# A log-sum-exp over heads: 2 MB loads, the bias of four heads added by TensorE in fp32, halves summed pairwise, last tile in pieces

## The chip, the cores and the metric

The program runs on one core of a Trainium2 chip. The metric is the device time of one execution in microseconds. A run over 1.5% above the fastest of the same kernel counts as slow.

## The reference

```python
B, S, D, H = 8, 2048, 2048, 8          # x: [8, 2048, 2048] fp32, bias: [8, 256] fp32
x_heads = x.reshape(B, S, H, Dh).transpose(0, 2, 1, 3) + bias[None, :, None, :]
x_tiled = np.repeat(x_heads, 2, axis=2)
mx = x_tiled.max(axis=-1, keepdims=True)
lse = mx.squeeze(-1) + np.log(np.exp(x_tiled - mx).sum(axis=-1))
```

For each row and head, 256 numbers are added to a bias, exponentiated and summed; the logarithm of the sum is written twice. The input is 134 MB and is read once, so the kernel is mostly a long stream of loads. Neither kernel subtracts the maximum.

## The kernel before

A tile is 128 rows of 2048 numbers (1 MB). Seven heads go one way: ScalarE takes the exponential in place, VectorE multiplies by exp(bias) and sums. The eighth head goes another way: TensorE adds the bias in PSUM (two bf16 products, reading the upper halves of the fp32 words), and ScalarE exponentiates and sums.

```python
XIN_BUFS = 8
for b in range(B):
    for sblk in range(nsblk):                               # 16 tiles of 1 MB
        xt = xin.tile([P, D], mybir.dt.float32, name="xt")
        nc.sync.dma_start(out=xt, in_=x[b, s0 : s0 + P, :])
        for h in range(n_ttr, H):                           # n_ttr = 7: one head
            ps = pspool.tile([P, Dh], mybir.dt.float32, name="ps")
            nc.tensor.matmul(ps, lhsT=ones_bf[0:1, :], rhs=b_hi, start=True, stop=False)
            nc.tensor.matmul(ps, lhsT=ident_bf[:, :], rhs=x_hi, start=False, stop=True)
            nc.scalar.activation(out=ps, in_=ps, func=ACT.Exp, accum_out=R[...])
        nc.scalar.activation(out=xt[:, 0 : 7 * Dh], in_=xt[:, 0 : 7 * Dh], func=ACT.Exp)
        for h in range(7):
            nc.vector.tensor_tensor_reduce(out=junk, in0=xt[:, sl], in1=w_rep[:, sl],
                op0=ALU.mult, op1=ALU.add, accum_out=R[...], ...)
    nc.tensor.transpose(out=ps, in_=R[:, b]..., identity=ident)   # once per batch
    nc.scalar.activation(out=res, in_=ps_view, func=ACT.Ln)
    # ... store
```

The order of instructions on each engine is not the order of this text: a scheduler decides it.

The softmax here doesn't subtract the row's maximum and nothing guards it: scores larger than these inputs give would overflow.

Of the kernel before, what the change touches and what calls it, by code (L numbers as in the profile page):

```python
# [8 lines left out]

N_TTR_HEADS = 7  # L10

XIN_BUFS = 8


@with_exitstack
def kernel(
    ctx: ExitStack,
    tc: tile.TileContext,
    x: bass.AP,
    bias: bass.AP,  # L20
    out: bass.AP,
):
    nc = tc.nc
    P = nc.NUM_PARTITIONS
    B, S, D = x.shape
    H, Dh = bias.shape
    assert D == H * Dh
    assert S % P == 0
    nsblk = S // P
    NCOL = H * nsblk  # L30
    assert NCOL <= P

    n_ttr = max(0, min(N_TTR_HEADS, H))
    ACT = mybir.ActivationFunctionType
    ALU = mybir.AluOpType

    const = ctx.enter_context(tc.tile_pool(name="const", bufs=1))
    rpool = ctx.enter_context(tc.tile_pool(name="rpool", bufs=1))
    xin = ctx.enter_context(tc.tile_pool(name="xin", bufs=XIN_BUFS))
    junkp = ctx.enter_context(tc.tile_pool(name="junkp", bufs=2))  # L40
    pspool = ctx.enter_context(tc.tile_pool(name="pspool", bufs=3, space=bass.MemoryType.PSUM))
    pspoolw = ctx.enter_context(tc.tile_pool(name="pspoolw", bufs=2, space=bass.MemoryType.PSUM))
    tpsum = ctx.enter_context(tc.tile_pool(name="tpsum", bufs=2, space=bass.MemoryType.PSUM))
    resp = ctx.enter_context(tc.tile_pool(name="resp", bufs=2))

    with tc.high_priority():
        act_sets = list(get_activation_tables(nc.m.arch).items())
        for set_idx, (_set_name, funcs) in enumerate(act_sets):
            if ACT.Exp in funcs and ACT.Ln in funcs:
                nc.scalar.add_instruction(  # L50
                    mybir.InstLoadActFuncSet(
                        name=nc.get_next_instruction_name(),
                        act_func_set_id=set_idx,
                    )
                )
                break

        ident = const.tile([P, P], mybir.dt.float32, name="ident")
        make_identity(nc, ident)
        ident_bf = const.tile([P, P], mybir.dt.bfloat16, name="ident_bf")  # L60
        make_identity(nc, ident_bf)
        ones_bf = const.tile([1, P], mybir.dt.bfloat16, name="ones_bf")
        nc.vector.memset(ones_bf, 1.0)  # L63

        brow = const.tile([1, D], mybir.dt.float32, name="brow")
        nc.scalar.dma_start(
            out=brow, in_=bias.rearrange("h j -> (h j)").unsqueeze(0)
        )
        w_rep = const.tile([P, D], mybir.dt.float32, name="w_rep")
        brb = brow.bitcast(mybir.dt.bfloat16)  # L70
        WCH = 512
        for c in range(D // WCH):
            b_hi_c = bass.AP(
                tensor=brb.tensor,
                offset=brb.offset + 2 * c * WCH + 1,
                ap=[[brb.ap[0][0], 1], [2, WCH]],
            )
            psw = pspoolw.tile([P, WCH], mybir.dt.float32, name="psw")
            nc.tensor.matmul(  # L79
                psw, lhsT=ones_bf[0:1, :], rhs=b_hi_c, start=True, stop=True  # L80
            )
            nc.scalar.activation(  # L82
                out=w_rep[:, c * WCH : (c + 1) * WCH], in_=psw, func=ACT.Exp
            )

    R = rpool.tile([P, B, H, nsblk], mybir.dt.float32, name="R")

    for b in range(B):
        for sblk in range(nsblk):
            s0 = sblk * P  # L90
            xt = xin.tile([P, D], mybir.dt.float32, name="xt")
            nc.sync.dma_start(out=xt, in_=x[b, s0 : s0 + P, :])

            if n_ttr < H:
                xb = xt.bitcast(mybir.dt.bfloat16)
                bb = brow.bitcast(mybir.dt.bfloat16)
            for h in range(n_ttr, H):
                x_hi = bass.AP(
                    tensor=xb.tensor,
                    offset=xb.offset + 2 * h * Dh + 1,  # L100
                    ap=[xb.ap[0], [2, Dh]],
                )
                b_hi = bass.AP(
                    tensor=bb.tensor,
                    offset=bb.offset + 2 * h * Dh + 1,
                    ap=[[bb.ap[0][0], 1], [2, Dh]],
                )
                ps = pspool.tile([P, Dh], mybir.dt.float32, name="ps")
                nc.tensor.matmul(  # L109
                    ps, lhsT=ones_bf[0:1, :], rhs=b_hi, start=True, stop=False  # L110
                )
                nc.tensor.matmul(  # L112
                    ps, lhsT=ident_bf[:, :], rhs=x_hi, start=False, stop=True
                )
                nc.scalar.activation(  # L115
                    out=ps,
                    in_=ps,
                    func=ACT.Exp,
                    accum_out=R[:, b, h, sblk : sblk + 1],
                )  # L120

            if n_ttr > 0:
                nc.scalar.activation(  # L123
                    out=xt[:, 0 : n_ttr * Dh],
                    in_=xt[:, 0 : n_ttr * Dh],
                    func=ACT.Exp,
                )
                for h in range(n_ttr):
                    sl = slice(h * Dh, (h + 1) * Dh)
                    junk = junkp.tile([P, Dh], mybir.dt.float32, name="junk")  # L130
                    nc.vector.tensor_tensor_reduce(  # L131
                        out=junk,
                        in0=xt[:, sl],
                        in1=w_rep[:, sl],
                        scale=1.0,
                        scalar=0.0,
                        op0=ALU.mult,
                        op1=ALU.add,
                        accum_out=R[:, b, h, sblk : sblk + 1],
                    )  # L140

        ps = tpsum.tile([NCOL, P], mybir.dt.float32, name="tps")
        nc.tensor.transpose(  # L143
            out=ps, in_=R[:, b].rearrange("p h s -> p (h s)"), identity=ident
        )
        res = resp.tile([NCOL, P, 2], mybir.dt.float32, name="res")
        ps_view = bass.AP(
            tensor=ps.tensor,
            offset=ps.offset,
            ap=[ps.ap[0], [1, P], [0, 2]],  # L150
        )
        nc.scalar.activation(out=res, in_=ps_view, func=ACT.Ln)  # L152
        ov = bass.AP(
            tensor=out.tensor,
            offset=out.offset + b * H * 2 * S,
            ap=[[2 * P, NCOL], [1, 2 * P]],
        )
        out_eng = nc.sync if b == B - 1 else nc.gpsimd
        out_eng.dma_start(out=ov, in_=res.rearrange("p s e -> p (s e)"))  # L159


# [28 lines left out]
```

## Time and profile before

| | before |
|---|---|
| time, median of the runs beside the changed kernel | 347.40 us |
| profiled span | 345.5 us |
| VectorE busy | 92% |
| ScalarE busy | 79% |
| load rate in the steady part | about 421 GB/s |
| last load complete at (its last packet ended at 336.7) | 337.2 us |

From the page of the kernel before: busy time per engine, then the span in 40 slices, each digit the busy tenths of a slice.

```profile
PE 95.0 (28%) x268; PEld 27.6 (8%) x268; DVE 316.6 (92%) x1793; ACT 272.4 (79%) x397; POOL 5.0 (1%) x15
...
DVE  0899989899898998999989989899899998999985
ACT  4978878788787887878778878788777887878872
...
DMA  7999999999999999999999999999999999999700
GB/s 303 427 421 421 417 422 423 422 421 421 419 423 417 424 421 419 423 420 424 423 418 418 424 420 423 421 422 419 422 416 412 370 401 424 420 411 409 286 24 15
```

The loads never rest, and VectorE (DVE) is nearly full. Which of the two is the bound is told by who waits. From the groups of instructions (busy us, mean ns of one, then the idle time just before them and who ended it):

```profile
L131 DVE CUSTOM_DVE_ANT_0 junk<-xt,w_rep 128x256 f32<-128x256 f32 x896 | 316.3, 422 | 24.0 <-ACT xt L123 15.4
L123 ACT ACTIVATE xt<-xt 128x1792 f32<-128x1792 f32 x128 | 217.2, 1698 | 62.7 <-DMA xt<-in_x_dram 56.2
```

VectorE waits for ScalarE, and ScalarE waits 56 us for loads: the loads bound the kernel. From the timeline of the end (start us, duration us, instruction, idle time before it and what ended it):

```profile
331.34 1.70 ACT L123 ACTIVATE xt<-xt 128x1792 f32<-128x1792 f32 x1 [0.38 <-DMA xt<-in_x_dram]
...
334.78 1.70 ACT L123 ACTIVATE xt<-xt 128x1792 f32<-128x1792 f32 x1 [1.35 <-DMA xt<-in_x_dram]
...
337.24 1.70 ACT L123 ACTIVATE xt<-xt 128x1792 f32<-128x1792 f32 x1 [0.37 <-DMA xt<-in_x_dram]
```

Tiles arrive 2.46 us apart, but one gap here is 3.44 us. Such gaps come about every 22 us. In the packets of the trace, an 8 KB instruction fetch goes ahead of each, and one load packet then takes 0.97 us in place of 0.31. After the last landing the kernel needs some 8 us more.

### The profile page before, as it was taken

Reading aid. Unit: us, or ns where it says so; the run is one execution under the profiler, and the core shown is the slowest. Engines: PE = TensorE matmul, PEld = TensorE weight load, DVE = VectorE, ACT = ScalarE, POOL = GpSimd, SP = SyncE. Lnnn points to the kernel's source line nnn. Section 1 sums busy time; section 2 is a strip of 40 time slices with the busy share of each in tenths; the row PEclk is TensorE's granted clock in tenths of the full one; section 3 lists DMA queues with packets and bytes.
Section 4 is the critical chain, followed back from the end, with each engine's and each line's share of the span. In section 5 each row is a group of like instructions: output and inputs, shape, how many; then the busy total and the mean of one; then the engine's idle time right before and its main releaser. Section 6 shows DMA issues by size and latency. Waiting matters only on the chain. (4 is left out here: it accounts for less than half of the span.)

```text
span 345.5 us, 3541 instructions
## 1 busy us (share of the span) xinstructions
PE 95.0 (28%) x268; PEld 27.6 (8%) x268; DVE 316.6 (92%) x1793; ACT 272.4 (79%) x397; POOL 5.0 (1%) x15
## 2 busy tenths in 40 slices
PE   2423223223322323322332322232223232222220
PEld 0100000000000000000010000000000000000000
DVE  0899989899898998999989989899899998999985
ACT  4978878788787887878778878788777887878872
POOL 1000000000000000000000000000000000000000
DMA  7999999999999999999999999999999999999700
GB/s 303 427 421 421 417 422 423 422 421 421 419 423 417 424 421 419 423 420 424 423 418 418 424 420 423 421 422 419 422 416 412 370 401 424 420 411 409 286 24 15
DMA packets 18939, 135.50 MB, mean 392 GB/s; under 512 B 2177, under 2 KB 2305, under 8 KB 2529
## 3 DMA queue, kind: packets, MB, share of 16 engines
q1 hardware_dynamic: 18576, 134.36, 94.3%
q0 software_dynamic: 336, 0.92, 0.7%
q14 instruction: 23, 0.19, 0.1%
q8 instruction: 2, 0.03, 0.0%
q10 hardware_dynamic: 2, 0.01, 0.0%
HBM read 134.23 MB, written 1.05 MB: 392 GB/s over the span
## 5 line engine op out<-in xcount | busy, mean ns | idle before, releaser
L131 DVE CUSTOM_DVE_ANT_0 junk<-xt,w_rep 128x256 f32<-128x256 f32 x896 | 316.3, 422 | 24.0 <-ACT xt L123 15.4
L123 ACT ACTIVATE xt<-xt 128x1792 f32<-128x1792 f32 x128 | 217.2, 1698 | 62.7 <-DMA xt<-in_x_dram 56.2
L109 PE MATMUL ps<-brow,ones_bf 1*128 1x256 bf16 x128 | 46.9, 368 | 207.6 <-ACT ps L115 207.5
L131 DVE DVE_READ_ACCUMULATOR2_ANT R<- 128x1 f32 x896 | 74.8, 83 | 0.0
L112 PE MATMUL ps<-xt,ident_bf 128*128 128x256 bf16 x128 | 49.3, 385 | 21.4 <-DMA xt<-in_x_dram 21.3
L115 ACT ACTIVATE ps<-ps 128x256 f32<-128x256 f32 x128 | 47.2, 369 | 0.0
L112 PEld LDWEIGHTS <-ident_bf 128*128 128x128 bf16 x128 | 13.2, 104 | 245.2 <-issue 245.2
L115 ACT ACTIVATION_READ_ACCUMULATOR ps<-ps 128x1 f32 x128 | 23.5, 184 | 0.0
L109 PEld LDWEIGHTS <-ones_bf 1*128 1x128 bf16 x128 | 12.5, 98 | 45.6 <-issue 45.6
L152 ACT ACTIVATE res<-tps 128x256 f32<-128x256 f32 x8 | 3.1, 383 | 6.6 <-PE tps L143 6.6
L159 POOL DMA_DIRECT2D out_dram<-res x7 | 3.9, 562 | 295.9 <-ACT res L152 295.9
L143 PE MATMUL tps<-ident,R 128*128 128x128 f32 x8 | 3.6, 452 | 13.8 <-DVE R L131 13.8
L79 PE MATMUL psw<-brow,ones_bf 1*128 1x512 bf16 x4 | 2.4, 601 | 4.2 <-DMA brow<-in_bias_dram 2.4
L143 PEld LDWEIGHTS tps<-ident,R 128*128 128x128 f32 x8 | 1.4, 180 | 19.3 <-issue 15.8
L82 ACT ACTIVATE w_rep<-psw 128x512 f32<-128x512 f32 x4 | 2.3, 593 | 0.0
L50 ACT ACT_TABLE_LOAD x1 | 1.3, 1283 | 0.7 <-PEq L174 0.7
L63 DVE MEMSET ones_bf<- 1x128 bf16 x1 | 0.2, 165 | 0.8 <-PEq L174 0.8
L79 PEld LDWEIGHTS <-ones_bf 1*128 1x128 bf16 x4 | 0.5, 118 | 4.0 <-issue 3.0
masks.py:199 POOL TENSOR_SCALAR_AFFINE_SELECT ident<-ident 128x128 f32<-128x128 f32 x1 | 0.3, 285 | 0.0
masks.py:199 POOL TENSOR_SCALAR_AFFINE_SELECT ident_bf<-ident_bf 128x128 bf16<-128x128 bf16 x1 | 0.3, 285 | 0.0
masks.py:197 POOL MEMSET ident<- 128x128 f32 x1 | 0.2, 205 | 0.3 <-POOLq L174 0.3
masks.py:197 POOL MEMSET ident_bf<- 128x128 bf16 x1 | 0.2, 206 | 0.0
(4 smaller groups left out, 0.4 us busy)
## 6 DMA issues: line engine op xcount, KB each, us to landing
xt<-in_x_dram SPq DMA_DIRECT2D x128, 1024.0 KB, 16.4
out_dram<-res POOLq DMA_DIRECT2D x7, 128.0 KB, 5.8
out_dram<-res SPq DMA_DIRECT2D x1, 128.0 KB
brow<-in_bias_dram ACTq DMA_DIRECT2D x1, 8.0 KB
```

The source lines that it names most:

```text
L50: nc.scalar.add_instruction(mybir.InstLoadActFuncSet(name=nc.get_next_instruction_name(), act_func_set_id=set_idx,))
L63: nc.vector.memset(ones_bf, 1.0)
L79: nc.tensor.matmul(psw, lhsT=ones_bf[0:1, :], rhs=b_hi_c, start=True, stop=True)
L82: nc.scalar.activation(out=w_rep[:, c * WCH : (c + 1) * WCH], in_=psw, func=ACT.Exp)
L109: nc.tensor.matmul(ps, lhsT=ones_bf[0:1, :], rhs=b_hi, start=True, stop=False)
L112: nc.tensor.matmul(ps, lhsT=ident_bf[:, :], rhs=x_hi, start=False, stop=True)
L115: nc.scalar.activation(out=ps, in_=ps, func=ACT.Exp, accum_out=R[:, b, h, sblk : sblk + 1],)
L123: nc.scalar.activation(out=xt[:, 0 : n_ttr * Dh], in_=xt[:, 0 : n_ttr * Dh], func=ACT.Exp,)
L131: nc.vector.tensor_tensor_reduce(out=junk, in0=xt[:, sl], in1=w_rep[:, sl], scale=1.0, scalar=0.0, op0=ALU.mult, op1=ALU.add, accum_out=R[ ...
L143: nc.tensor.transpose(out=ps, in_=R[:, b].rearrange("p h s -> p (h s)"), identity=ident)
L152: nc.scalar.activation(out=res, in_=ps_view, func=ACT.Ln)
L159: out_eng.dma_start(out=ov, in_=res.rearrange("p s e -> p (s e)"))
```

## The change

Its intent: load 2 MB at a time with two rows per partition, so that each packet is longer; take work from VectorE by letting TensorE add the bias of four heads exactly (the fp32 data times an fp32 identity, and the bias split into three bf16 parts), so that VectorE sums their two halves pairwise in half the elements; load the last tile in pieces to shorten the end.

```diff
-N_TTR_HEADS = 7
-XIN_BUFS = 8
+K = 2
+NPE = 4
+XIN_BUFS = 9
 ...
+    pbias = ... tc.tile_pool(name="pbias", bufs=3, space=bass.MemoryType.PSUM)
+        # bias split into three bf16 parts by GpSimd, moved to b3 by three small DMAs
+        nc.gpsimd.tensor_copy(bparts[:, 0], bp)
+        nc.gpsimd.tensor_sub(brest[:, 0], bp, bparts[:, 0])
+        ...
+    def biased(xt, b, blk, k):
+        ps = pbias.tile([P, CPE], F32, name="ps")
+        for c in range(0, CPE, MM):                     # CPE = 1024, MM = 512
+            nc.tensor.matmul(ps[:, c : c + MM], lhsT=ones3, rhs=b3[:, c : c + MM],
+                start=True, stop=False)
+        for c in range(0, CPE, MM):
+            nc.tensor.matmul(ps[:, c : c + MM], lhsT=ident, rhs=xt[:, k, c : c + MM],
+                start=False, stop=True)
+        nc.scalar.activation(out=xt[:, k, 0:CPE], in_=ps, func=ACT.Exp)
+        for h in range(NPE):                            # halves, 128 elements
+            nc.vector.tensor_tensor_reduce(out=junk[:, 0:HALF], in0=xt[:, k, c : c + HALF],
+                in1=xt[:, k, c + HALF : c + Dh], op0=ALU.add, op1=ALU.add, ...)
 ...
+            if not last:
+                nc.sync.dma_start(out=xt, in_=xb[blk])              # 2 MB
+                nc.scalar.activation(out=xt[:, :, CPE:D], in_=xt[:, :, CPE:D], func=ACT.Exp)
+                for k in range(K):
+                    biased(xt, b, blk, k)
+                for k in range(K):
+                    for h in range(NPE, H):
+                        weigh(xt, b, blk, k, h)                     # as before, 256 elements
+            else:
+                # the same in five pieces: 2 x 512 KB for TensorE's heads, 512 KB, 2 x 256 KB
```

More of the change, by code (lines that the diff above doesn't have):

```diff
@@ L8 @@
 from concourse.masks import make_identity
-N_TTR_HEADS = 7
-XIN_BUFS = 8
+F32 = mybir.dt.float32
+BF16 = mybir.dt.bfloat16
+ACT = mybir.ActivationFunctionType
+ALU = mybir.AluOpType
+K = 2
+NPE = 4
+XIN_BUFS = 9
 @with_exitstack
@@ L26 @@
     H, Dh = bias.shape
-    assert D == H * Dh
-    assert S % P == 0
-    nsblk = S // P
-    NCOL = H * nsblk
-    assert NCOL <= P
-    n_ttr = max(0, min(N_TTR_HEADS, H))
-    ACT = mybir.ActivationFunctionType
-    ALU = mybir.AluOpType
+    assert D == H * Dh and S % (P * K) == 0
+    NBLK = S // (P * K)
+    NW = H - NPE
+    CPE = NPE * Dh
+    CW = NW * Dh
+    MM = 512
+    HALF = Dh // 2
     const = ctx.enter_context(tc.tile_pool(name="const", bufs=1))
-    rpool = ctx.enter_context(tc.tile_pool(name="rpool", bufs=1))
     xin = ctx.enter_context(tc.tile_pool(name="xin", bufs=XIN_BUFS))
     junkp = ctx.enter_context(tc.tile_pool(name="junkp", bufs=2))
-    pspool = ctx.enter_context(tc.tile_pool(name="pspool", bufs=3, space=bass.MemoryType.PSUM))
-    pspoolw = ctx.enter_context(tc.tile_pool(name="pspoolw", bufs=2, space=bass.MemoryType.PSUM))
-    tpsum = ctx.enter_context(tc.tile_pool(name="tpsum", bufs=2, space=bass.MemoryType.PSUM))
-    resp = ctx.enter_context(tc.tile_pool(name="resp", bufs=2))
+    pbias = ctx.enter_context(
+        tc.tile_pool(name="pbias", bufs=3, space=bass.MemoryType.PSUM)
+    )
+    tpsum = ctx.enter_context(
+        tc.tile_pool(name="tpsum", bufs=2, space=bass.MemoryType.PSUM)
+    )
+    resp = ctx.enter_context(tc.tile_pool(name="resp", bufs=2))
+    brow = const.tile([1, D], F32, name="brow")
+    w_rep = const.tile([P, CW], F32, name="w_rep")
+    ident = const.tile([P, P], F32, name="ident")
+    ones = const.tile([1, P], F32, name="ones")
+    ones3 = const.tile([3, P], BF16, name="ones3")
+    b3 = const.tile([3, CPE], BF16, name="b3")
+    bparts = const.tile([1, 3, CPE], BF16, name="bparts")
+    brest = const.tile([1, 2, CPE], F32, name="brest")
+    R = const.tile([P, B, K, H, NBLK], F32, name="R")
     with tc.high_priority():
-        act_sets = list(get_activation_tables(nc.m.arch).items())
-        for set_idx, (_set_name, funcs) in enumerate(act_sets):
+        for set_idx, (_name, funcs) in enumerate(
+            get_activation_tables(nc.m.arch).items()
+        ):
             if ACT.Exp in funcs and ACT.Ln in funcs:
@@ L56 @@
                 break
-        ident = const.tile([P, P], mybir.dt.float32, name="ident")
-        make_identity(nc, ident)
-        ident_bf = const.tile([P, P], mybir.dt.bfloat16, name="ident_bf")
-        make_identity(nc, ident_bf)
-        ones_bf = const.tile([1, P], mybir.dt.bfloat16, name="ones_bf")
-        nc.vector.memset(ones_bf, 1.0)
-        brow = const.tile([1, D], mybir.dt.float32, name="brow")
         nc.scalar.dma_start(
@@ L68 @@
         )
-        w_rep = const.tile([P, D], mybir.dt.float32, name="w_rep")
-        brb = brow.bitcast(mybir.dt.bfloat16)
-        WCH = 512
-        for c in range(D // WCH):
-            b_hi_c = bass.AP(
-                tensor=brb.tensor,
-                offset=brb.offset + 2 * c * WCH + 1,
-                ap=[[brb.ap[0][0], 1], [2, WCH]],
-            )
-            psw = pspoolw.tile([P, WCH], mybir.dt.float32, name="psw")
-            nc.tensor.matmul(
-                psw, lhsT=ones_bf[0:1, :], rhs=b_hi_c, start=True, stop=True
-            )
-            nc.scalar.activation(
-                out=w_rep[:, c * WCH : (c + 1) * WCH], in_=psw, func=ACT.Exp
-            )
@@ L86 @@
-    R = rpool.tile([P, B, H, nsblk], mybir.dt.float32, name="R")
-    for b in range(B):
-        for sblk in range(nsblk):
-            s0 = sblk * P
-            xt = xin.tile([P, D], mybir.dt.float32, name="xt")
-            nc.sync.dma_start(out=xt, in_=x[b, s0 : s0 + P, :])
-            if n_ttr < H:
-                xb = xt.bitcast(mybir.dt.bfloat16)
-                bb = brow.bitcast(mybir.dt.bfloat16)
-            for h in range(n_ttr, H):
-                x_hi = bass.AP(
-                    tensor=xb.tensor,
-                    offset=xb.offset + 2 * h * Dh + 1,
-                    ap=[xb.ap[0], [2, Dh]],
-                )
-                b_hi = bass.AP(
-                    tensor=bb.tensor,
-                    offset=bb.offset + 2 * h * Dh + 1,
-                    ap=[[bb.ap[0][0], 1], [2, Dh]],
-                )
-                ps = pspool.tile([P, Dh], mybir.dt.float32, name="ps")
-                nc.tensor.matmul(
-                    ps, lhsT=ones_bf[0:1, :], rhs=b_hi, start=True, stop=False
-                )
-                nc.tensor.matmul(
-                    ps, lhsT=ident_bf[:, :], rhs=x_hi, start=False, stop=True
-                )
-                nc.scalar.activation(
-                    out=ps,
-                    in_=ps,
-                    func=ACT.Exp,
-                    accum_out=R[:, b, h, sblk : sblk + 1],
-                )
-            if n_ttr > 0:
-                nc.scalar.activation(
-                    out=xt[:, 0 : n_ttr * Dh],
-                    in_=xt[:, 0 : n_ttr * Dh],
-                    func=ACT.Exp,
-                )
-                for h in range(n_ttr):
-                    sl = slice(h * Dh, (h + 1) * Dh)
-                    junk = junkp.tile([P, Dh], mybir.dt.float32, name="junk")
-                    nc.vector.tensor_tensor_reduce(
-                        out=junk,
-                        in0=xt[:, sl],
-                        in1=w_rep[:, sl],
-                        scale=1.0,
-                        scalar=0.0,
-                        op0=ALU.mult,
-                        op1=ALU.add,
-                        accum_out=R[:, b, h, sblk : sblk + 1],
-                    )
-        ps = tpsum.tile([NCOL, P], mybir.dt.float32, name="tps")
-        nc.tensor.transpose(
-            out=ps, in_=R[:, b].rearrange("p h s -> p (h s)"), identity=ident
-        )
-        res = resp.tile([NCOL, P, 2], mybir.dt.float32, name="res")
-        ps_view = bass.AP(
-            tensor=ps.tensor,
-            offset=ps.offset,
-            ap=[ps.ap[0], [1, P], [0, 2]],
-        )
-        nc.scalar.activation(out=res, in_=ps_view, func=ACT.Ln)
@@ new lines @@
+        nc.vector.memset(ones, 1.0)
+        nc.vector.memset(ones3, 1.0)
+        make_identity(nc, ident)
+        psw = pbias.tile([P, CW], F32, name="ps")
+        for c in range(0, CW, MM):
+            nc.tensor.matmul(
+                psw[:, c : c + MM],
+                lhsT=ones,
+                rhs=brow[:, CPE + c : CPE + c + MM],
+                start=True,
+                stop=True,
+            )
+        nc.scalar.activation(out=w_rep, in_=psw, func=ACT.Exp)
+        bp = brow[:, 0:CPE]
@@ new lines @@
+        nc.gpsimd.tensor_copy(bparts[:, 0], bp)
+        nc.gpsimd.tensor_sub(brest[:, 0], bp, bparts[:, 0])
+        nc.gpsimd.tensor_copy(bparts[:, 1], brest[:, 0])
+        nc.gpsimd.tensor_sub(brest[:, 1], brest[:, 0], bparts[:, 1])
+        nc.gpsimd.tensor_copy(bparts[:, 2], brest[:, 1])
+        for i in range(3):
+            nc.gpsimd.dma_start(out=b3[i : i + 1, :], in_=bparts[:, i])
+    def biased(xt, b, blk, k):
+        ps = pbias.tile([P, CPE], F32, name="ps")
+        for c in range(0, CPE, MM):
+            nc.tensor.matmul(
+                ps[:, c : c + MM],
+                lhsT=ones3,
+                rhs=b3[:, c : c + MM],
+                start=True,
+                stop=False,
+            )
+        for c in range(0, CPE, MM):
+            nc.tensor.matmul(
+                ps[:, c : c + MM],
+                lhsT=ident,
+                rhs=xt[:, k, c : c + MM],
+                start=False,
+                stop=True,
+            )
+        nc.scalar.activation(out=xt[:, k, 0:CPE], in_=ps, func=ACT.Exp)
+        for h in range(NPE):
+            c = h * Dh
+            junk = junkp.tile([P, Dh], F32, name="junk")
+            nc.vector.tensor_tensor_reduce(
+                out=junk[:, 0:HALF],
+                in0=xt[:, k, c : c + HALF],
+                in1=xt[:, k, c + HALF : c + Dh],
+                scale=1.0,
+                scalar=0.0,
+                op0=ALU.add,
+                op1=ALU.add,
+                accum_out=R[:, b, k, h, blk : blk + 1],
+            )
@@ new lines, in weigh @@
+    def weigh(xt, b, blk, k, h):
+        c = h * Dh
+        junk = junkp.tile([P, Dh], F32, name="junk")
+        nc.vector.tensor_tensor_reduce(
+            out=junk,
+            in0=xt[:, k, c : c + Dh],
+            in1=w_rep[:, c - CPE : c - CPE + Dh],
+            scale=1.0,
+            scalar=0.0,
+            op0=ALU.mult,
+            op1=ALU.add,
+            accum_out=R[:, b, k, h, blk : blk + 1],
+        )
+    for b in range(B):
+        xb = x[b].rearrange("(n p k) d -> n p k d", p=P, k=K)
+        for blk in range(NBLK):
+            xt = xin.tile([P, K, D], F32, name="xt")
+            last = b == B - 1 and blk == NBLK - 1
+            if not last:
+                nc.sync.dma_start(out=xt, in_=xb[blk])
+                nc.scalar.activation(
+                    out=xt[:, :, CPE:D], in_=xt[:, :, CPE:D], func=ACT.Exp
+                )
+                for k in range(K):
[4 more added lines that the diff above has]
+            else:
+                pieces = [(k, 0, CPE) for k in range(K)]
+                pieces += [(k, CPE, D) for k in range(K - 1)]
+                pieces += [(K - 1, CPE + i * MM, CPE + (i + 1) * MM) for i in range(CW // MM)]
+                for k, c0, c1 in pieces:
+                    nc.sync.dma_start(
+                        out=xt[:, k, c0:c1], in_=xb[blk, :, k, c0:c1]
+                    )
+                for k, c0, c1 in pieces:
+                    if c0 < CPE:
+                        biased(xt, b, blk, k)
+                        continue
+                    for c in range(c0, c1, MM):
+                        nc.scalar.activation(
+                            out=xt[:, k, c : c + MM],
+                            in_=xt[:, k, c : c + MM],
+                            func=ACT.Exp,
+                        )
+                        for h in range(c // Dh, (c + MM) // Dh):
+                            weigh(xt, b, blk, k, h)
+        NR = H * NBLK
+        tps = tpsum.tile([NR, K, P], F32, name="tps")
+        for k in range(K):
+            nc.tensor.transpose(
+                out=tps[:, k],
+                in_=R[:, b, k].rearrange("p h n -> p (h n)"),
+                identity=ident,
+            )
+        res = resp.tile([NR, P, K, 2], F32, name="res")
+        tv = bass.AP(
+            tensor=tps.tensor,
+            offset=tps.offset,
+            ap=[tps.ap[0], [1, P], [P, K], [0, 2]],
+        )
+        nc.scalar.activation(out=res, in_=tv, func=ACT.Ln)
@@ L155 @@
             offset=out.offset + b * H * 2 * S,
-            ap=[[2 * P, NCOL], [1, 2 * P]],
+            ap=[[2 * K * P, NR], [1, 2 * K * P]],
         )
         out_eng = nc.sync if b == B - 1 else nc.gpsimd
-        out_eng.dma_start(out=ov, in_=res.rearrange("p s e -> p (s e)"))
+        out_eng.dma_start(out=ov, in_=res.rearrange("p s k e -> p (s k e)"))
 _INS = ['x', 'bias']
```

## The prediction

> **What bounds it now.** The loads, and among the 16 DMA engines the slowest one. The slices show 421 GB/s and DMA at 9 tenths nearly throughout; the page has VectorE 92% busy, ScalarE 79%. ScalarE's big exponentials start 2.48 us apart (1 MB at 421 GB/s), except about every 22 us, when the gap is 3.45 us. In the trace's packets an instruction fetch (8 KB, 0.33 us) precedes each such gap, and one 8 KB load packet then takes 0.97 us in place of 0.31. The engine that carries these fetches falls behind: 15 of the 16 parts of the last tile land by 327.8 us, the last at 337.2 us. VectorE needs 7 x 0.346 = 2.42 us per tile: just hidden. After the last landing the tail is 8.3 us: 4.3 to VectorE's end, 4 for transpose, Ln and store.
>
> **What changes, per 256 rows (2 MB).**
> - DMA: packets of 16 KB, if the contiguous run becomes one packet. Packets here take 0.0475 us (1 KB), 0.161 (4 KB), 0.311 (8 KB): about 10 ns fixed each. Estimate 0.611 us for 16 KB, so the last engine needs 512 x 0.611 = 313 us where it took 1024 x 0.311 = 318.5: 5.7 us less. VectorE has 2,052 instruction rows for 1,795, so two or three more fetches of about 1 us. The last landing moves to about 333 us.
> - VectorE: 8 full reductions of 0.346 us, and 8 half ones, estimated at 0.346 minus 128 elements at the rate of 0.267 us per 256, about 0.213. Sum 4.47 us, was 4.84.
> - ScalarE: about 3.8 us (from 1.70 us per 1,792 elements), was 4.3.
> - TensorE becomes heavy: 4 fp32 matmuls of 512 columns and 4 bf16 ones. The Trainium skill (FP8 and Floating Point Precision, TensorE Precision Notes) gives true fp32 four passes; its page TensorE: Matmul & The Clock Gate, Part 1, gives 2.4 GHz after some 3.4 us of sustained work and 1.2 GHz before. This trace shows neither for fp32 products. Estimate from these pages: 4 x 0.86 + 4 x 0.22 = 4.3 us warm, 8.5 us cold.
>
> **Critical path.** With three bias buffers, the changed order puts a bias matmul that waits for the previous tile's last ScalarE step ahead of the next tile's fp32 matmuls. That closes a loop: 0.43 (bias) + 3.4 (fp32) + about 1.2 (exponential and hand-over) = about 5.05 us per 2 MB, against 5.15 for the loads with fetch stalls. TensorE is nearly a second bound, so a late start (bias split on GpSimd, about 14 us) is recovered slowly.
>
> The tail does not shrink, despite the pieces: VectorE still has most of the preceding 2 MB tile to do when the last piece lands. I estimate 8 us from last landing to VectorE's end (was 4.3), then 4.5. So 333 + 12.5 = 345.5 span, 347 measured at most; overlap may be better.
>
> **Prediction: 345 us, 80% range 337 to 356. Faster by over 2%: 0.25; within 2%: 0.57; slower: 0.18.**
>
> **Right if** the packets are 16 KB and take about 0.61 us; the last landing is near 333 us; fetch stalls stay about 1 us; TensorE is busy for 80% or more; half reductions are 0.21 us apart; VectorE works 7 us or more after the last landing.
>
> **Wrong if** fp32 matmuls take longer than 0.86 us (a loop of 5.5 us gives 370 us and starving loads); TensorE stays cold (over 500 us); fp32 matmuls are faster or larger packets stream better than estimated, with a short tail (336 to 340 us); packets stay 8 KB (about 350 us).

## The result, and the profile after

The changed kernel took 381.71 us (380.85 to 382.86, four fast runs) against 347.40 us. The ratio is 1.0993, with a 95% interval of 1.0972 to 1.1014: 10% slower. A ratio here is the mean time of one kernel's fast runs over that of the other's of the same rounds, so it is not quite the ratio of the quoted medians.

From the page of the changed kernel, with one more row: PEclk is the TensorE clock that was granted, in tenths of full speed.

```profile
PE 319.1 (84%) x788; PEld 112.1 (29%) x788; DVE 292.6 (77%) x2050; ACT 252.4 (66%) x205; POOL 13.2 (3%) x21
...
PE   3299998889879888888978998798888888888990
...
PEclk9999999999999999899999999999999999999997
DMA  8999999999999999999999999999999999940000
GB/s 310 435 431 427 426 424 430 431 422 431 425 430 425 426 427 430 428 425 423 399 390 344 399 389 366 379 388 374 395 393 387 380 377 393 327 170 1 0 1 14
```

VectorE and ScalarE have less to do, as intended, and the loads run at about 427 GB/s for the first half. From about 180 us on they fall below 400: the buffers have filled, and loads wait until one is free. In the last four slices there are no loads at all (the 14 is the store). The groups:

```profile
L116 PE MATMUL ps<-xt,ident 128*128 128x512 f32 x512 | 245.6, 617 | 0.0
L123 ACT ACTIVATE xt<-ps 128x1024 f32<-128x1024 f32 x128 | 130.9, 1023 | 107.1 <-PE ps L116 107.1
L127 DVE CUSTOM_DVE_ANT_0 junk<-xt 128x128 f32<-128x128 f32 x512 | 118.6, 287 | 82.0 <-ACT xt L123 81.7
...
L159 ACT ACTIVATE xt<-xt 128x2048 f32<-128x2048 f32 x63 | 119.8, 1902 | 11.8 <-DMA xt<-in_x_dram 11.8
...
L108 PE MATMUL ps<-b,ones 3*128 3x512 bf16 x256 | 76.7, 379 | 43.1 <-ACT xt L123 32.2
...
L192 PE MATMUL tps<-ident,R 128*64 128x128 f32 x16 | 5.1, 322 | 11.2 <-DVE R L141 11.2
```

The chain of waiting has turned round. ScalarE's wait for loads is down from 56 to 12 us; it waits 107 us for TensorE. And TensorE, which is busy for 84% only, waits 32 us for ScalarE, always ahead of a bias product (L108). It also waits 11.2 us for VectorE ahead of the transposes (L192): 4.9 us of that at the very end of the kernel, 6.3 us at the seven batch ends before. The end of the chain that ended last (start us, us, what):

```profile
335.86 3.65 PE ps L116 x8
339.53 1.03 ACT xt L123
340.61 0.59 PE ps L108 x2
341.19 3.65 PE ps L116 x8
```

This is a loop. One round is 5.33 us (335.86 to 341.19), and it handles one tile of 2 MB, which the loads bring in 4.89 us (8 packets of 0.611 us on each DMA engine) between instruction fetches. TensorE's timeline shows why the loop is closed:

```profile
202.75 0.59 PE L108 MATMUL ps<-b,ones 3*128 3x512 bf16 x2 [0.58 <-ACT xt L123]
203.27 3.70 PE L116 MATMUL ps<-xt,ident 128*128 128x512 f32 x8
206.90 0.60 PE L108 MATMUL ps<-b,ones 3*128 3x512 bf16 x2
208.08 0.59 PE L108 MATMUL ps<-b,ones 3*128 3x512 bf16 x2 [0.58 <-ACT xt L123]
208.60 3.70 PE L116 MATMUL ps<-xt,ident 128*128 128x512 f32 x8
```

Three bias buffers exist. The scheduler put two pairs of bias products ahead of each tile's eight fp32 products; the second pair belongs to the tile after. Its buffer is the one that the previous tile's last exponential still reads, so TensorE stands still until ScalarE has finished. Only then may it take the data products of a tile that has long landed.

The first tiles are different: TensorE starts late, when the split bias arrives, at half clock, and in another order.

```profile
16.97 1.01 PE L108 MATMUL ps<-b,ones 3*128 3x512 bf16 x2 [10.77 <-DMA b<-bparts]
17.91 3.78 PE L116 MATMUL ps<-xt,ident 128*128 128x512 f32 x4
21.63 1.03 PE L108 MATMUL ps<-b,ones 3*128 3x512 bf16 x2
22.59 3.78 PE L116 MATMUL ps<-xt,ident 128*128 128x512 f32 x4
26.30 0.60 PE L108 MATMUL ps<-b,ones 3*128 3x512 bf16 x2
26.83 1.98 PE L116 MATMUL ps<-xt,ident 128*128 128x512 f32 x4
28.74 0.60 PE L108 MATMUL ps<-b,ones 3*128 3x512 bf16 x2
...
```

Here each group's bias products stand directly ahead of its own data products, and at full clock one group takes 2.44 us (26.30 to 28.74), a tile 4.89 us, without a standstill. That is the same work in 0.44 us less per tile.

### The profile page after: what moved, and what is told of

It reads as the page before. It is cut to its first block, busy times and chain, and to the rows that moved or that the text cites. A ratio compares the mean times of both kernels' runs of the same rounds, so it can differ in the third digit from the quotient of the medians.

```text
span 379.9 us, 4224 instructions
## 1 busy us (share of the span) xinstructions
PE 319.1 (84%) x788; PEld 112.1 (29%) x788; DVE 292.6 (77%) x2050; ACT 252.4 (66%) x205; POOL 13.2 (3%) x21
## 5 line engine op out<-in xcount | busy, mean ns | idle before, releaser
L116 PE MATMUL ps<-xt,ident 128*128 128x512 f32 x512 | 245.6, 617 | 0.0
L123 ACT ACTIVATE xt<-ps 128x1024 f32<-128x1024 f32 x128 | 130.9, 1023 | 107.1 <-PE ps L116 107.1
L127 DVE CUSTOM_DVE_ANT_0 junk<-xt 128x128 f32<-128x128 f32 x512 | 118.6, 287 | 82.0 <-ACT xt L123 81.7
L141 DVE CUSTOM_DVE_ANT_0 junk<-xt,w_rep 128x256 f32<-128x256 f32 x512 | 181.8, 419 | 0.0
L159 ACT ACTIVATE xt<-xt 128x2048 f32<-128x2048 f32 x63 | 119.8, 1902 | 11.8 <-DMA xt<-in_x_dram 11.8
L116 PEld LDWEIGHTS ps<-xt,ident 128*128 128x128 f32 x512 | 92.2, 193 | 114.8 <-issue 114.8
L108 PE MATMUL ps<-b,ones 3*128 3x512 bf16 x256 | 76.7, 379 | 43.1 <-ACT xt L123 32.2
L108 PEld LDWEIGHTS <-ones 3*128 3x128 bf16 x256 | 18.3, 92 | 121.5 <-issue 114.1
L127 DVE DVE_READ_ACCUMULATOR2_ANT R<- 128x1 f32 x512 | 41.9, 82 | 0.0
L141 DVE DVE_READ_ACCUMULATOR2_ANT R<- 128x1 f32 x512 | 41.6, 81 | 0.0
L192 PE MATMUL tps<-ident,R 128*64 128x128 f32 x16 | 5.1, 322 | 11.2 <-DVE R L141 11.2
L192 PEld LDWEIGHTS tps<-ident,R 128*64 128x64 f32 x16 | 1.8, 112 | 23.8 <-DVE R L141 23.8
```

The source lines that it names most:

```text
L108: nc.tensor.matmul(ps[:, c : c + MM], lhsT=ones3, rhs=b3[:, c : c + MM], start=True, stop=False,)
L116: nc.tensor.matmul(ps[:, c : c + MM], lhsT=ident, rhs=xt[:, k, c : c + MM], start=False, stop=True,)
L123: nc.scalar.activation(out=xt[:, k, 0:CPE], in_=ps, func=ACT.Exp)
L127: nc.vector.tensor_tensor_reduce(out=junk[:, 0:HALF], in0=xt[:, k, c : c + HALF], in1=xt[:, k, c + HALF : c + Dh], scale=1.0, scalar=0.0, ...
L141: nc.vector.tensor_tensor_reduce(out=junk, in0=xt[:, k, c : c + Dh], in1=w_rep[:, c - CPE : c - CPE + Dh], scale=1.0, scalar=0.0, op0=ALU. ...
L159: nc.scalar.activation(out=xt[:, :, CPE:D], in_=xt[:, :, CPE:D], func=ACT.Exp)
```

## The experiments

Theory A: the loop TensorE, ScalarE, TensorE sets the time. Rivals: the 2 MB loads (B), the sheer number of TensorE passes (C), the late start, or the end.

**1. Products swapped** (data first, bias second, so no bias product can be pulled ahead).

```diff
-   # bias product: start=True, stop=False; then data product: start=False, stop=True
+   # data product: start=True, stop=False; then bias product: start=False, stop=True
```

> The changed kernel with the two products of each group swapped: data times identity first, bias second, same instructions in number and shape, so no bias product that waits for ScalarE stands ahead of the next tile's fp32 products. Theory A (a loop TensorE -> ScalarE -> TensorE of 5.33 us per 2 MB, with 64 tiles of it, sets the time): the loop opens, TensorE runs back to back at 4.89 us per tile as it does for the first tiles of the changed kernel, and the time falls to 350 us (345 to 358). Rival B (the 2 MB loads or the bigger buffers are what is slow): no change, 375 us or more. Rival C (the sheer number of TensorE passes, not the wait, sets it): no change either, and TensorE stays as busy, 84%.

Measured: 365.55 us (one of the four runs, 374.56 us, was slow), ratio of the fast runs 1.0508. Half of the loss is gone, so B and C as stated fall; but 350 was expected. In steady stretches TensorE did run back to back at 4.89 us per tile. The shortfall is seen where a batch ends:

```profile
54.26 0.30 PE L192 MATMUL tps<-ident,R 128*64 128x128 f32 x1 [1.56 <-DVE R L141]
...
56.10 0.42 PE L192 MATMUL tps<-ident,R 128*64 128x128 f32 x1
56.32 1.91 PE L108 MATMUL ps<-xt,ident 128*128 128x512 f32 x2
58.16 1.03 PE L116 MATMUL ps<-b,ones 3*128 3x512 bf16 x2
59.12 3.73 PE L108 MATMUL ps<-xt,ident 128*128 128x512 f32 x4
```

The transposes of a finished batch wait for VectorE in TensorE's queue. After the standstill of 1.56 us four fp32 records (a product of 512 fp32 columns has two in the trace) take 3.73 us where they took 1.98: the granted clock was at half from 55.8 to 62.7 us, and so it was after the next four batches. After the two batches that followed, standstills of the same length left it at full.

**2. No bias products** (four heads wrong).

```diff
-        for c in range(0, CPE, MM):
-            nc.tensor.matmul(ps[:, c : c + MM], lhsT=ones3, rhs=b3[:, c : c + MM], ...)
```

> The changed kernel without the bias products (four heads wrong on purpose; the split bias is still prepared). TensorE has 3.65 us of work per 2 MB and neither the loop nor the wait for the split bias at the start. Theory A: bound by the loads again, last landing at about 331 us, time 345 us (338 to 350). Rival B: 375 us or more, as the loads are untouched.

Measured: 348.19 us, ratio 1.0032 (relative error 0.054). The same 2 MB loads, and ScalarE's and VectorE's work unchanged: B falls. The last load ended at about 334 us, and the tail after it was over 12 us, so even with the loads as the bound there is no gain over the kernel before.

**3. Bias without the split**, truncated to bf16, ready at once.

```diff
-                lhsT=ones3,               rhs=b3[:, c : c + MM],
+                lhsT=ones3[0:1, :],       rhs=b_hi(c),   # upper halves of the bias row
```

> The changed kernel with the bias taken, truncated to bf16, straight from the bias row as in the kernel before: no splitting on GpSimd, no small DMAs; the bias products keep their number, shape and place. Theory A: the loop stays at 5.33 us per tile, but TensorE's first tile starts at about 7.7 us, when the first tile lands, in place of 17.0: 9 us less, 372 us (370 to 375). If the loads set the time the start costs nothing: 380 to 383 us.

Measured: 371.96 us, ratio 1.0707: 9.75 us less than the changed kernel. The first fp32 product starts 9.2 us earlier (8.67 us in place of 17.91), and the half clock of the start ends sooner too (11.7 us in place of 26.2). While the loop is the bound, a late start is not made good.

**4. The kernel before with 2 MB loads** (the layout of the sums, and two transposes per batch in place of one, follow from two rows per partition; nothing else).

```diff
-            xt = xin.tile([P, D], ...);     nc.sync.dma_start(out=xt, in_=x[b, s0 : s0 + P, :])
+            xt2 = xin.tile([P, K, D], ...); nc.sync.dma_start(out=xt2, in_=xbk[blk])
```

> The kernel before with nothing but its loads changed to 2 MB, two rows per partition (8 buffers of 2 MB). Theory A: the loads are not what slowed the changed kernel: packets of 16 KB at 0.611 us, last landing about 332 us, VectorE then has up to two halves of a tile left; time 343 to 350 us, near 347. Rival B: over 365 us.

Measured: 346.03 us, ratio 0.9961 (0.9946 to 0.9976), which counts as the same at 2%. The loads end at 332.3 us in place of 336.7, a gain of 4.4 us. The tail takes 11.9 us in place of 8.8 (span less the end of the last load) and eats 3.1 of it. The load size was never what slowed the changed kernel.

**5. Products swapped, TensorE's order pinned, transposes three tiles later.**

```diff
+    with tc.manual_schedule(engines={mybir.EngineType.PE}):
         for b in range(B):
             ...
+            if blk == 3 and b > 0:
+                finish(b - 1)             # transposes, Ln and store of the batch before
```

> The kernel of the swapped products, with TensorE's order pinned to the program's and the two transposes of a batch put three tiles later, so that TensorE does not stand still waiting for VectorE at the end of a batch. The last run fell short (365.5 us for 350 expected) with the granted clock at 0.6 in one or two of the slices after each batch end. If the standstill at the transposes is what lowers the clock: no dips, TensorE back to back at 4.89 us per tile from about 9 us on, loads as the near second bound, time 347 us (344 to 352). If the clock falls for another reason: dips stay, 360 us or more.

Measured: 350.04 us, ratio 1.0078, as expected. The granted clock stayed at full after the start, against five low slices inside run 1; first the row of run 1's page, then that of this run's.

```profile
PEclk9999996999969999699997999899999999999996
```

```profile
PEclk9969999999999999999999999999999999999997
```

**6. Three heads on TensorE instead of four**, the loop kept (the steps of 512 columns are fitted to 768; not shown).

```diff
-NPE = 4
+NPE = 3
```

> The changed kernel with three heads on TensorE in place of four; its order, with the bias product ahead of the next tile's products, stays. Theory A: the loop is as long as what is in it: 0.45 (bias) + 2.74 (fp32) + 0.9 (exponential and hand-over) = 4.1 us, below the 4.89 us of a 2 MB load, so the loads bound again and the late start is made good: 346 us (343 to 350), last landing at about 332 us. Rival (late start or load size set the time, not the loop): 365 us or more.

Measured: 360.58 us; ratio of the fast runs 1.0368 (two of six runs, the profiled one too, were slow). Missed: 346 was expected. In that slow profile the loop has the length expected, 4.16 us from one bias standstill to the next. I had left out the transposes. They waited 52 us for VectorE (nine times, up to 8.5 us), and the clock dropped after each batch. With less work on TensorE, VectorE is the one behind, and TensorE stands still for it. This is read from the slow profile; of the fast runs the record shows only that they missed too, at a mean clock of 0.91.

**7. The same with the last tile loaded whole.**

```diff
-            last = b == B - 1 and blk == NBLK - 1
+            last = False
```

> The kernel with three heads, and its last tile loaded whole like the others, in a kernel that the loads bound. If pieces shorten the tail as intended, this is 3 us or more slower than with pieces. My view that VectorE's backlog, not the size of the last piece, makes the tail: within 1.5 us of it.

Measured: ratio of the fast runs 1.0376, against 1.0368 with pieces (two of the four runs were slow). No difference can be seen, but this kernel turned out not to be bound by its loads, so it doesn't say what pieces are worth in one that is.

**8. A combination**: three heads, swapped products, orders pinned, late transposes, the last five tiles in 1 MB halves.

```diff
+    ordered = {PE, Activation, DVE}; data product first; finish(b - 1) two tiles later
+    # last five tiles: 1 MB loads, and ScalarE sums three heads of each first half
```

> A version from the findings: three heads on TensorE, data product before bias product, orders of TensorE, ScalarE and VectorE pinned, transposes two tiles later, VectorE's weighted heads before the halved ones, the last five tiles loaded in 1 MB halves with three heads of each first half summed by ScalarE. If the loads bound at 4.89 us per 2 MB plus fetch stalls and VectorE's backlog is what makes the tail, the last landing stays near 332 us and the tail falls from about 14 to about 9: 342 us (338 to 346).

Measured: 351.38 us, from 347.73 to 358.52 (two of the six runs were slow); ratio of the fast runs 1.0067. Missed: 342 was expected. The granted clock was 0.81 in the profiled run (slow) and 0.87 to 0.91 in the five others; roughly, the slower runs had the lower clock. Why it stays low longer in this kernel is open.

**9. The changed kernel with TensorE's order pinned and late transposes, nothing swapped.**

```diff
+    with tc.manual_schedule(engines={mybir.EngineType.PE}):   # bias, then its own data
+            if blk == 3 and b > 0:
+                finish(b - 1)
```

> The changed kernel with nothing but TensorE's order pinned to the program's: each bias product directly ahead of the data products of its own group, never ahead of another tile's, and the transposes three tiles later. Bias first, as in the changed kernel, so the late start at about 17 us stays. Theory A: the loop alone is opened. TensorE then needs 17.0 + 9.3 (first tile, cold) + 63 x 4.89 = 334.4 us and some 4 us of transposes; with the tail 351 us (348 to 356), near the 350.0 us of the run that also swapped the products. If the late start is what costs, not the loop: 372 us or more.

Measured: 349.45 us, ratio 1.0060 (1.0044 to 1.0077). Not one instruction was taken away, and the bias is still late; order alone, the later transposes included, gives back 32.3 of the 34.3 us. The timeline of TensorE shows no standstill from 18.1 to 339.5 us, and a group takes 2.45 us:

```profile
202.29 1.98 PE L116 MATMUL ps<-xt,ident 128*128 128x512 f32 x4
204.20 0.60 PE L108 MATMUL ps<-b,ones 3*128 3x512 bf16 x2
204.73 1.98 PE L116 MATMUL ps<-xt,ident 128*128 128x512 f32 x4
206.65 0.60 PE L108 MATMUL ps<-b,ones 3*128 3x512 bf16 x2
```

With the loop open, TensorE's own work has become the bound of this run. The chain that ended last, by engine:

```profile
PE 92%; POOL 2%; DMA 2%; DVE 1%; ACT 0%; issue 0%; DVEq 0%
```

So C is not gone, only smaller: 4.89 us of TensorE per tile is as long as the loads' packets. In run 5 the same chain leads back to a load. There TensorE is three groups ahead of this run at 33 us and yet ends no earlier, so the late start no longer costs anything that can be seen.

**10. The loop made again by hand**, to see whether the order or the late transposes gave it back.

```diff
-                    for k in range(K):
-                        biased(xt, b, blk, k)            # bias and data of one group
+                    ps1 = bias_ahead()                   # bias of this tile's second group
+                    ps_next = bias_ahead()               # bias of the next tile's first
+                    biased(xt, b, blk, 0, ps0)           # data only
+                    biased(xt, b, blk, 1, ps1)
+                    ps0 = ps_next
```

> The kernel with the pinned order (349.5 us), with the changed kernel's order written out by hand: the second bias product of a tile and the first of the next tile ahead of the tile's data products. Everything else, the late transposes too, stays. Theory A: 5.33 us per tile come back: 17 + 64 x 5.33 and the tail, less the waits at the transposes: 374 us (368 to 382). If what the pinning gained came from the transposes' place: 352 us or less.

Measured: 462.73 us, ratio 1.3317, far over the 374 expected. The loop was longer than meant: the scheduler had put the next tile's big exponential (1.90 us) between the two exponentials that TensorE waits for. A round took 6.3 us with a standstill of 1.57 us, and the clock fell at intervals. ScalarE's order belongs to the loop, and I had not looked at it.

**11. The same with ScalarE's order pinned to that of the changed kernel.** Before this run it was open whether the order alone explains the 5.33 us.

```diff
-    with tc.manual_schedule(engines={mybir.EngineType.PE}):
+    with tc.manual_schedule(engines={mybir.EngineType.PE, mybir.EngineType.Activation}):
```

> The kernel with the changed kernel's TensorE order written out by hand (462.7 us), and ScalarE's order pinned as well to what the changed kernel and the pinned kernel have: big exponential, then the two exponentials of the same tile. Theory A: one tile takes 0.52 (bias) + 3.70 (fp32) + 1.02 (exponential) + 0.09 = 5.33 us as in the changed kernel; with the late start, the cold first tile and the tail 374 us (368 to 382), the clock at full after the start. If the order is not the cause of those 5.33 us: 349 to 355 us, as with the pinned order.

Measured: 371.47 us, ratio 1.0712. The loop is back, 5.33 us from 207.73 to 213.06:

```profile
207.73 3.70 PE L119 MATMUL ps<-xt,ident 128*128 128x512 f32 x8
211.37 0.60 PE L108 MATMUL ps<-b,ones 3*128 3x512 bf16 x2
212.54 0.59 PE L108 MATMUL ps<-b,ones 3*128 3x512 bf16 x2 [0.58 <-ACT xt L126]
213.06 3.27 PE L119 MATMUL ps<-xt,ident 128*128 128x512 f32 x7
```

So closing the loop costs 22.0 us (371.47 less 349.45; from 200 to 212 us ScalarE takes one big exponential and two small ones in turn in both). The other 10.2 us between this and the changed kernel's 381.71 go with what still differs, and no run separates it. One part is the place of the transposes: between batches TensorE waited 6.3 us for VectorE in the changed kernel and not at all here. Another is the clock: it was at half until 26.2 us and again from 152.5 to 155.9 us there, here only until 23.1 us.

**12. Transposes directly after their batch**, order pinned, no loop.

```diff
-            if blk == 3 and b > 0:
+            if blk == 0 and b > 0:
```

> The kernel with the pinned order (349.5 us), with the two transposes of a batch directly after its last tile in place of three tiles later; nothing else. If TensorE's standstill there costs itself and then lowers the granted clock: about 5 us of waiting for VectorE and several us at half clock, at each of seven batch ends: 395 us (375 to 415), the clock at 0.5 after each. If the place does not matter: 350 us.

Measured: 405.36 us, ratio 1.1677. From TensorE's timeline at the first batch end:

```profile
56.02 1.98 PE L116 MATMUL ps<-xt,ident 128*128 128x512 f32 x4
61.48 0.30 PE L156 MATMUL tps<-ident,R 128*64 128x128 f32 x1 [3.47 <-DVE R L141]
62.86 0.42 PE L156 MATMUL tps<-ident,R 128*64 128x128 f32 x1 [1.08 <-DVE R L141]
63.21 1.03 PE L108 MATMUL ps<-b,ones 3*128 3x512 bf16 x2
64.17 3.78 PE L116 MATMUL ps<-xt,ident 128*128 128x512 f32 x4
```

Two small transposes per batch, moved by three tiles, are worth 56 us: a standstill of 4.6 us, then 7 to 10 us at half clock, at each of seven batch ends.

**13. A version without fp32 products**: the kernel of run 4, with the last six tiles in 1 MB halves.

```diff
+TAIL = 6
+                n_ttr = H - 2 if tail and k == 0 else H - 1     # one more head on ScalarE
+                if tail and not (left == 1 and k == K - 1):
+                    nc.sync.dma_start(out=xt2[:, k], in_=xbk[blk, :, k])
+                elif tail:                                      # last half in three pieces
+                    for c0, c1 in ((7 * Dh, D), (0, 5 * Dh), (5 * Dh, 7 * Dh)):
+                        nc.sync.dma_start(out=xt2[:, k, c0:c1], in_=xbk[blk, :, k, c0:c1])
```

> A version without the fp32 products: the kernel before with 2 MB loads (346.0 us), its last six tiles loaded in 1 MB halves, two heads in place of one summed by ScalarE in each first half of them, and the last half in three pieces, the last with two heads. If the last landing stays near 332.5 us and VectorE has no more than about 3.5 us left then, in place of 7.5: 342.5 us (340 to 345), 1.4% faster than the kernel before. If pieces and halves do not shorten VectorE's backlog: 345 to 347 us.

Measured: 343.97 us (343.91 to 344.02), ratio 0.9905 (0.9891 to 0.9920). This is the fastest kernel: clear of the noise, but within the 2% that count as the same as the kernel before. Loads end at 332.9 us, and the tail is 9.1 us in place of 11.9. That lies in the expected range of 340 to 345, above its centre of 342.5: VectorE still had 4.4 us to do after the last piece.

## Why the prediction was wrong

The prediction was 345 us with a range to 356; it took 381.7.

- **The step that failed: "TensorE is nearly a second bound", "about 5.05 us per 2 MB, against 5.15 for the loads".** The loop was found ahead of time, and its mechanism is shown by runs 9 and 11. Its size was off. The bias pair took 0.52 us for 0.43: its two records stand 0.215 us apart, but from the second to the first fp32 record it is 0.30. The fp32 products took 3.70 for 3.4: their records stand 0.43 us apart as estimated, except that the first takes 0.53, and the last 0.59 until it has ended; a loop pays both each round. ScalarE's share was 1.02 + 0.09, slightly under the 1.2 estimated. The sum is 5.33 us, more than the loads' 5.15, so the loop was the bound; 64 rounds of 0.28 us more are 18 us.
- **The sum was made along one path only.** "So 333 + 12.5 = 345.5" follows the loads. By my own numbers TensorE's path was already longer: a start at 14 us, 64 rounds of 5.05 us and a tail of 12.5 make 350 us, before the cold first tile. A late start is "recovered slowly" only if the loop is faster than the loads; in a loop that is the bound it is never recovered. Run 3 shows 9.75 us for a start 9.2 us earlier and a stretch at half clock that ends earlier.
- **Waits at the transposes were not thought of at all.** They are in the middle of TensorE's queue and wait for VectorE: 6.3 us between batches here, and in run 12, with the half clock that followed, as much as 56 us.
- **Right:** packets of 16 KB take 0.611 us, to the nanosecond of the estimate. With the loop open, the loads ended at 333.7 us (run 9), "about 333" as predicted; in the changed kernel itself at 337.6 us. The half reductions are 0.21 us apart. The Trainium skill (FP8 and Floating Point Precision, TensorE Precision Notes) has four passes for true fp32: this trace agrees in time, with two records of 0.43 us for each product of 512 columns, 0.86 us, which is four times the 0.215 us between the two bf16 records of the same width.
- **Right, too, but partly by luck: the end does not get shorter.** In run 9 it is 15.0 us after the last load, longer than the 12.5 predicted. The prediction had put this down to VectorE's backlog; in run 9 TensorE is still at work until 339.5 us, 5.7 us after the last load, and VectorE follows it. So even the changed work in the best order tried (349.45 us) gains nothing: 3 us of earlier loads go to a tail that is 6 us longer.

The saving on VectorE (24 us of busy time) was off the critical path up to the last tile, since the loads bound the kernel before.

## What to carry to other kernels

When a change gives work to an idle engine, follow one buffer of the new work round: who fills it, who frees it, and what stands in the queue between. If an instruction that waits for the buffer is placed ahead of work that is ready, the latencies of both engines add up to a period, and this period, not the busy share, is to be set against the bound. Sum every engine's path from its own start to the end, and look at the real order of each engine in the loop before believing a schedule; pinning the order and moving the transposes were worth 32 us here without removing an instruction.

## What the Trainium skill lacked or had wrong

- TensorE: Matmul & The Clock Gate, Part 1, has full clock after some 3.4 us of sustained work. Here TensorE worked without a gap and full clock came after 9.3 us in the changed kernel (16.97 to 26.23) and 13.8 us in run 9 (18.11 to 31.95). In the profile of run 8, a slow run, the clock was full at 14.8 us, fell to half at 18.25 and stayed there for 37.6 us of work without a gap (to 55.8). What decides this is open.
- The same page, in its table "Why this matters for your kernels", advises no idle gaps over about 3 us. Shorter ones were not safe here: of seven gaps of about 1.56 us (run 1) five were followed by half clock, and so was, at intervals, one of 1.57 us per tile (run 10); gaps of 0.58 us per tile (run 11) were not. In the changed kernel, with the same gaps and seven of 0.7 us at batch ends, half clock came once, for 3.4 us.
- No page tells what an instruction fetch does to a stream of loads (it belongs to Runtime: NRT & Kernel Launch, Instruction fetch mechanics): in the kernel before, one load packet after it took 0.97 us in place of 0.31, about every 22 us. Of the 16 parts of the last tile 15 had landed by 327.8 us, and the tile waited for the last one until 337.2.
- In DMA: Bandwidth & Descriptors I found no time for load packets of this size: 0.311 us for 8 KB and 0.611 us for 16 KB, so twice the length saved 11 ns in 622.
